# An encoder trunk in split float32: where the rounded high part of each weight comes from for the second sequence

## The chip, the cores and the metric

The kernel runs on one core of a Trainium2 chip. The metric is the device time of one execution in microseconds (us); a result is the median of several runs. The engines are TensorE (PE, with PEld for its weight loads), VectorE (DVE), ScalarE (ACT), GpSimd (POOL) and SyncE (SP). SP computes nothing here: its queue issues nearly all DMA transfers, in order, and waits before each until what the transfer needs is there.

## The reference

A trunk of two layers is applied to two requests of 512 tokens and 1024 channels, with one set of weights. Cut to what matters:

```python
def encoder_trunk(x, p):
    for l in range(DEPTH):                                   # 2
        h = rms_norm(x, p['ln1_g'][l])
        z = h @ p['w_in'][l]                                 # 1024 x 2816
        z_s5, z_hy, z_rw, z_na = jnp.split(z, IN_SPLITS, axis=-1)
        ...                                                  # four mixers, 256 channels each
        groups = [rms_norm(y, p['grp_g'][l, i]) for i, y in enumerate((y_s5, y_hy, y_rw, y_na))]
        x = x + jnp.concatenate(groups, axis=-1) @ p['w_out'][l]         # 1024 x 1024
        h = rms_norm(x, p['ln2_g'][l])
        x = x + jnp.square(jax.nn.relu(h @ p['w_mlp1'][l])) @ p['w_mlp2'][l]   # 1024 x 4096 x 1024
    return x

def reference(x_prompt, x_sample, ...):
    return (encoder_trunk(x_prompt, p), encoder_trunk(x_sample, p))
```

The mixers are a diagonal state-space scan (S5), a long convolution (Hyena), a linear-attention recurrence in two directions (RWKV-7) and 2-D neighbourhood attention.

## The kernel before

**Dense layers.** All tensors lie with channels on the 128 partitions and the 512 tokens of one sequence along the free dimension. To multiply with float32 accuracy, every operand is split: the high part is the value rounded to the matmul type float32r, the low part is what the rounding left. `mm3` (lines 1432 to 1434) makes three matmuls of 128x128 by 128x512 for each block: high weight by high activation, high weight by low activation, low weight by high activation. `dense` sums eight such blocks in one PSUM bank, `w_out` and `second` in `mlp` four or eight.

**Weights.** `load_w` brings four blocks, 128 x 512 float32 or 256 KB, so that one weight load serves 12 matmuls. A layer has 44 loads for `w_in`, 16 for `w_out`, and 128 for the two matrices of the MLP: 188, and 376 in the two layers. The first sequence meets each weight first, and the second meets it again later.

- First time (lines 1418 to 1422): SP loads the raw weights into a slot for low parts, ACT casts them into a slot for high parts (`split`, line 297), POOL, or VectorE for every fourth load, subtracts (line 298) and leaves the low part where the raw weights were, and SP writes the low part to DRAM (`lo`).
- Again (lines 1414 to 1416): SP loads the raw weights and the saved low part into two slots, and ACT casts the raw weights in place (line 1416).

There are seven slots of 256 KB. In the first case, three hold high parts and four hold low parts, in turn. In the second case, the loads take pairs of slots round the ring of seven. A slot is free when the matmuls that read it have ended, and a DMA that reads it too.

**Order.** Three streams of generators are interleaved: the dense layers of both sequences, the RWKV and S5 work with the other mixers, and the mixers of the very first sequence. A scheduler then orders the instructions of each engine, from a simulated time line and from priorities. The dense stream runs: `w_in` of layer 0 for sequence 0 (first time), for sequence 1 (again); `w_out`, MLP of layer 0 and `w_in` of layer 1 for sequence 0 (first time), the same for sequence 1 (again); `w_out` and MLP of layer 1 for sequence 0 (first time), and for sequence 1 (again). The last of these has no mixers beside it.

The profile's names: `m` is any SBUF buffer of the kernel's own allocator, weights among them; `pd` is the PSUM of the dense layers, `ra`, `ma` and `nm` that of the mixers and norms; `in_w_in`, `in_w_out` and `in_w_mlp` are the raw weights in DRAM, `lo` the saved low parts.

Of the kernel before, what the change touches and what calls it, by code (L numbers as in the profile page):

```python
# [5 lines left out]
F32 = mybir.dt.float32  # L6
F32R = mybir.dt.float32r
# [1392 lines left out]
def load_w(K, key):  # L1400


    nc = K.nc
    sh = [P, 4, P]
    src = K.A[key[0]][key[1:]]
    n = K.nw
    K.nw += 1
    again = key in K.lows
    i, j = (2 * n % NW, (2 * n + 1) % NW) if again else (n % NHI, NHI + n % (NW - NHI))
    hi, lo = (K.W.view(NMEM + 2 * o, sh, F32R) for o in (i, j))  # L1410
    raw = K.W.view(NMEM + 2 * (i if again else j), sh, F32)
    K.tc.cur_priority -= OFF_W
    if again:
        nc.sync.dma_start(out=raw, in_=src)
        nc.sync.dma_start(out=lo.bitcast(F32), in_=K.lows[key])
        nc.scalar.copy(out=hi, in_=raw)  # L1416
    else:
        nc.sync.dma_start(out=raw, in_=src)
        K.split(hi, lo, raw, nc.vector if K.nw % LO_V == 0 else nc.gpsimd)
        K.n += 1  # L1420
        d = K.lows[key] = K.d(sh, f"lo_{K.n}")
        nc.sync.dma_start(out=d, in_=lo.bitcast(F32))
    K.tc.cur_priority += OFF_W
    return hi, lo

# [12 lines left out]
def dense(K, key, h, tag="pd"):  # L1438

    w = [load_w(K, key + (kh,)) for kh in range(2)]  # L1440
    ps = K.p([P, S], tag)
    mm3(K, ps, [(w[k // 4][0][:, k % 4], w[k // 4][1][:, k % 4], h[k][0], h[k][1]) for k in range(8)])
    return ps
# [99 lines left out]
def w_out(K, l, khs, ys, xsrc, xp, done, M):  # L1543


    nc = K.nc
    load = not xp
    for m in range(8):
        if load and m % 2 == 0:
            xp.append(M([P, 2, S]))  # L1550
        x = xp[m // 2][:, m % 2]
        if load:
            nc.sync.dma_start(out=x, in_=xsrc[m * P:m * P + P])
        w = [load_w(K, ('w_out', l, m, kh)) for kh in khs]
        ps = K.p([P, S], "pd")
        mm3(K, ps, [(w[i][0][:, j], w[i][1][:, j]) + tuple(ys[HALVES[kh][j // 2]][:, part, j % 2] for part in range(2))
                    for i, kh in enumerate(khs) for j in range(4)])
        nc.vector.tensor_tensor(out=x, in0=ps, in1=x, op=ADD)
        if done:
            done(m, x, xp[m // 2])  # L1560
        yield
    M.free(*(ys.pop(g) for kh in khs for g in HALVES[kh]))


def mlp(K, l, h, R, x, done, M):
# [14 lines left out]
    def second(e):  # L1580
        for m in range(8):
            wh, wl = load_w(K, ('w_mlp2', l, m, e))
            ps = K.p([P, S], "pd")
            mm3(K, ps, [(wh[:, j], wl[:, j], hid[4 * e + j][:, 0], hid[4 * e + j][:, 1]) for j in range(4)])
            nc.vector.tensor_tensor(out=x[m], in0=ps, in1=x[m], op=ADD)  # L1585
            if e == 7:
                done(m, x[m])
            yield
        for j in range(4):
            M.free(hid.pop(4 * e + j))  # L1590
# [47 lines left out]
def trunk(tc, A, O):  # L1638
    nc = tc.nc
    base = place(nc)  # L1640
    with tc.tile_pool(name="sb", bufs=1) as sb, \
            tc.tile_pool(name="ps", bufs=1, space=bass.MemoryType.PSUM) as ps, \
            tc.tile_pool(name="dr", bufs=1, space=bass.MemoryType.DRAM) as dr:
        K = Ctx(tc, base, sb, ps, dr, A)
        K.s5w, K.hys, K.lows, K.nw, K.nz = {}, {}, {}, 0, 0
        K.W = K.mem()

        DM, MX = K.mem((0, DHI)), K.mem((DHI, NMEM))
# [170 lines left out]
NMEM, DHI, DLO, DS5 = 164, 84, 41, 144  # L1819

NW, NHI = 7, 3
# [49 lines left out]
```

## Time and profile before

| | |
|---|---|
| median of 3 runs | 3195.2 us (3182.29 to 3195.77) |
| the profiled execution | 3179.4 us, its span 3177.6 us |
| PE busy | 2951.0 us, 93% of the span |
| DVE, ACT, POOL busy | 1973.0, 1051.9, 828.9 us |
| casts of weights for the second sequence (line 1416) | 376, 232.8 us of ACT |
| DMA moved | 571.92 MB, a mean of 180 GB/s; 155.83 MB of it written to HBM |
| granted TensorE clock, mean | 0.95 |

Busy times overlap, so they don't add up to the span. Matmuls are pipelined, and one can be counted busy while the one before it still runs. What a stage is bound by is read from the stage: its PE idle time, its granted clock (1.00 is 2.4 GHz), its share of DMA time, and the waits that ended last.

### The profile page before, as it was taken

The page shows a single profiled execution, that of the slowest core. Times are in us where ns is not written, and L with a number is a line of the kernel's source. Part 1 is how long each engine was busy: PE and PEld are TensorE (multiplying, and loading weights), DVE is VectorE, ACT ScalarE, POOL GpSimd, SP SyncE. Part 2 cuts the span into 40 slices and gives each one's busy share as a digit, 9 for nine tenths or more (in the row PEclk, how much of TensorE's full clock was granted, in tenths as well). Part 3 has the DMA queues.
Part 4 walks back from the last instruction along what each step waited for, and adds up shares of the span by engine and source line. Part 5 has one row for each costly group of instructions (what it writes and reads, how often), then busy time and mean ns, then how long its engine had stood idle before and what let it go on. Part 6 is the DMA issues. An engine that isn't in the chain of part 4 may idle for free.

```text
span 3177.6 us, 48702 instructions
## 1 busy us (share of the span) xinstructions
PE 2951.0 (93%) x17328; PEld 2308.4 (73%) x17328; DVE 1973.0 (62%) x3755; ACT 1051.9 (33%) x1922; POOL 828.9 (26%) x693
## 2 busy tenths in 40 slices
PE   7987998798899998899899999998998999999999
PEld 5666776676677877767676778776776777778887
DVE  8888775785854768757627436765647457733332
ACT  5333233332322333333323223433322323332222
POOL 5642201432332336432001001312333223300000
PEclk9898999898999999999999999999999999999999
DMA  7577574365554546766655545577556445556565
GB/s 221 164 232 201 189 210 131 117 169 165 151 163 145 173 161 207 227 191 201 186 151 157 173 150 182 196 211 221 181 170 181 152 162 181 178 178 194 192 193 195
DMA packets 482840, 571.92 MB, mean 180 GB/s; under 512 B 187910, under 2 KB 238726, under 8 KB 481576
## 3 DMA queue, kind: packets, MB, share of 16 engines
q1 hardware_dynamic: 482600, 568.81, 58.4%
q8 instruction: 139, 2.28, 0.3%
q14 instruction: 101, 0.83, 0.1%
HBM read 409.95 MB, written 155.83 MB: 178 GB/s over the span
## 4 chain that ended last, share of the span: by engine, by line
PE 64%; DVE 16%; DMA 9%; issue 4%; SPq 3%; ACT 2%; POOL 1%; DVEq 0%; ACTq 0%; POOLq 0%
PE pd L1432 16%; PE pd L1434 16%; PE pd L1433 15%; DVE m L1195 2%; PE ra L677 2%; PE ra L675 2%; DMA m<-in_w_mlp 2%; PE ra L467 1%; DMA m<-in_w_in 1%; DVE m L864 1%; DVE m L530 1%; DVE m L298 1%; DMA m<-lo 1%; PE ra L1226 1%; PE ra L660 1%
## 5 line engine op out<-in xcount | busy, mean ns | idle before, releaser
L1432 PE MATMUL pd<-m,m 128*128 128x512 f32 x2984 | 1225.9, 412 | 91.7 <-ACT m L297 32.7
L1434 PE MATMUL pd<-m,m 128*128 128x512 f32 x2984 | 1210.2, 406 | 34.7 <-DMA m<-lo 23.6
L1433 PE MATMUL pd<-m,m 128*128 128x512 f32 x2984 | 1206.0, 404 | 2.3 <-DVE m L298 2.3
L1432 PEld LDWEIGHTS pd<-m,m 128*128 128x128 f32 x2984 | 580.4, 195 | 242.0 <-issue 46.0
L1434 PEld LDWEIGHTS pd<-m,m 128*128 128x128 f32 x2984 | 578.8, 194 | 176.0 <-DMA m<-lo 27.4
L1433 PEld LDWEIGHTS pd<-m,m 128*128 128x128 f32 x2984 | 580.6, 195 | 130.0 <-issue 8.0
L298 POOL TENSOR_TENSOR m<-m,m 128x512 fp32r<-128x512 f32 x282 | 395.7, 1405 | 736.5 <-ACT m L297 676.4
L1416 ACT CAST m<-m 128x512 fp32r<-128x512 f32 x376 | 232.8, 620 | 712.3 <-DMA m<-in_w_mlp 434.2
L297 ACT CAST m<-m 128x512 fp32r<-128x512 f32 (+1 forms) x400 | 256.9, 645 | 624.7 <-PE pd L1433 232.9
L1585 DVE TENSOR_TENSOR m<-pd,m 128x512 f32<-128x512 f32 x256 | 175.2, 686 | 262.6 <-PE pd L1434 262.2
L1575 DVE SCALAR_TENSOR_TENSOR do<-pd,R 128x512 f32<-128x512 f32 x128 | 87.7, 688 | 198.9 <-PE pd L1434 188.7
L1195 DVE TENSOR_TENSOR m<-m,m 128x512 f32<-128x512 f32 (+1 forms) x224 | 142.0, 677 | 4.5 <-POOL m L1195 3.6
L298 DVE TENSOR_TENSOR m<-m,m 128x512 fp32r<-128x512 f32 (+1 forms) x118 | 104.9, 889 | 62.9 <-ACT m L297 59.6
L298 DVE TENSOR_TENSOR m<-do,m 128x512 fp32r<-128x512 f32 x128 | 100.4, 786 | 62.1 <-ACT m L297 61.5
L297 ACT CAST m<-do 128x512 fp32r<-128x512 f32 x128 | 79.2, 620 | 137.0 <-DVE do L1576 136.8
L1576 DVE TENSOR_TENSOR do<-do 128x512 f32<-128x512 f32 x128 | 112.5, 880 | 3.0
L1456 POOL TENSOR_TENSOR m<-m 128x512 f32<-128x512 f32 x40 | 58.6, 1466 | 128.1 <-ACT m L1455 126.1
L1463 DVE SCALAR_TENSOR_TENSOR m<-m,par,m 128x512 fp32r<-128x512 f32 x64 | 65.1, 1026 | 34.2 <-ACT m L1462 34.1
L677 PE MATMUL ra<-m,m 128*64 128x64 f32 x512 | 77.8, 246 | 0.0
L1195 POOL TENSOR_TENSOR m<-m,m 128x512 f32<-128x512 f32 x32 | 49.2, 1540 | 98.1 <-DVE m L1195 54.9
L467 PEld LDWEIGHTS ra<-m,m 64*128 64x128 f32 x512 | 50.8, 201 | 32.5 <-issue 24.3
L675 PE MATMUL ra<-m,rw_st 64*64 64x64 f32 x448 | 73.8, 246 | 0.0
(359 smaller groups left out, 3489.9 us busy)
## 6 DMA issues: line engine op xcount, KB each, us to landing
m<-in_w_mlp SPq DMA_DIRECT2D x512, 256.0 KB, 2.9
lo<-m SPq DMA_DIRECT2D x376, 256.0 KB, 2.3
m<-lo SPq DMA_DIRECT2D x376, 256.0 KB, 2.7
m<-in_w_in SPq DMA_DIRECT2D x176, 256.0 KB, 3.5
m<-zr SPq DMA_DIRECT2D x36, 512.0 KB, 4.7
m<-in_w_out SPq DMA_DIRECT2D x64, 256.0 KB, 3.0
m<-in_xT SPq DMA_DIRECT2D x32, 256.0 KB, 4.5
zr<-do SPq DMA_DIRECT2D x32, 256.0 KB, 2.2
```

The costliest lines, as they stand in the source:

```text
L297: self.nc.scalar.copy(out=hi, in_=x)
L298: eng.tensor_tensor(out=lo, in0=x, in1=hi.bitcast(F32), op=SUB)
L675: nc.tensor.matmul(out=py[b0:b0 + 64, d, c], lhsT=st[b0:b0 + 64, d, c], rhs=ar[c][b0:b0 + 64, ch, 1], start=True, stop=False)
L677: nc.tensor.matmul(out=py[b0:b0 + 64, d, c], lhsT=uv[:, ch, c, q], rhs=sr[:, ch, 2 * c + q], start=st is None, stop=True)
L1195: eng.tensor_tensor(out=o, in0=a, in1=b, op=op)
L1416: nc.scalar.copy(out=hi, in_=raw)
L1432: K.nc.tensor.matmul(out=ps, lhsT=wh, rhs=hh, start=(i == 0), stop=False)
L1433: K.nc.tensor.matmul(out=ps, lhsT=wh, rhs=hl, start=False, stop=False)
L1434: K.nc.tensor.matmul(out=ps, lhsT=wl, rhs=hh, start=False, stop=(i == n - 1))
L1575: nc.vector.scalar_tensor_tensor(out=r, in0=ps, scalar=0.0, in1=R, op0=MAX, op1=MUL)
L1576: nc.vector.tensor_tensor(out=r, in0=r, in1=r, op=MUL)
L1585: nc.vector.tensor_tensor(out=x[m], in0=ps, in1=x[m], op=ADD)
```

## The change

The first sequence now writes both parts to DRAM, the high part (`hi`) as well as the low one, one store each on SP. The second sequence loads both parts from there and casts nothing. The raw weights are read once, by the first sequence. The slots and their order stay as they were: three and four in turn at the first time, pairs round the ring of seven again. The split of the first time is the same.

```diff
-    src = K.A[key[0]][key[1:]]
...
-    again = key in K.lows
-    i, j = (2 * n % NW, (2 * n + 1) % NW) if again else (n % NHI, NHI + n % (NW - NHI))
-    hi, lo = (K.W.view(NMEM + 2 * o, sh, F32R) for o in (i, j))
-    raw = K.W.view(NMEM + 2 * (i if again else j), sh, F32)
...
-    if again:
-        nc.sync.dma_start(out=raw, in_=src)
-        nc.sync.dma_start(out=lo.bitcast(F32), in_=K.lows[key])
-        nc.scalar.copy(out=hi, in_=raw)
+    if key in K.parts:
+        hi, lo = (K.W.view(NMEM + 2 * ((2 * n + i) % NW), sh, F32R) for i in range(2))
+        for t, d in zip((hi, lo), K.parts[key]):
+            nc.sync.dma_start(out=t.bitcast(F32), in_=d)
     else:
-        nc.sync.dma_start(out=raw, in_=src)
+        hi = K.W.view(NMEM + 2 * (n % NHI), sh, F32R)
+        o = NMEM + 2 * (NHI + n % (NW - NHI))
+        raw, lo = K.W.view(o, sh, F32), K.W.view(o, sh, F32R)
+        nc.sync.dma_start(out=raw, in_=K.A[key[0]][key[1:]])
         K.split(hi, lo, raw, nc.vector if K.nw % LO_V == 0 else nc.gpsimd)
         K.n += 1
-        d = K.lows[key] = K.d(sh, f"lo_{K.n}")
-        nc.sync.dma_start(out=d, in_=lo.bitcast(F32))
+        K.parts[key] = [K.d(sh, f"{p}_{K.n}") for p in ("hi", "lo")]
+        for t, d in zip((hi, lo), K.parts[key]):
+            nc.sync.dma_start(out=d, in_=t.bitcast(F32))
```

In the changed file the loads of the second sequence are line 1411, the raw load of the first is line 1416, both stores are line 1421, and the matmuls lines 1431 to 1433. SP's queue in the MLP of layer 1 for the first sequence, before (a name's last number only tells buffers apart):

```order
L1422 DMA lo_2191_23157<-m_23152 128x512
L1418 DMA m_23231<-in_w_mlp 128x512
L1422 DMA lo_2199_23202<-m_23197 128x512
L1418 DMA m_23239<-in_w_mlp 128x512
L1422 DMA lo_2203_23235<-m_23230 128x512
L1418 DMA m_23289<-in_w_mlp 128x512
```

And the changed kernel's, in the same stage:

```order
L1421 DMA hi_2519_23403<-m_23397 128x512
L1421 DMA lo_2520_23404<-m_23399 128x512
L1416 DMA m_23460<-in_w_mlp 128x512
L1421 DMA hi_2522_23413<-m_23407 128x512
L1421 DMA lo_2523_23414<-m_23409 128x512
L1416 DMA m_23470<-in_w_mlp 128x512
```

Load and store alternated; now a load is followed by the high and then the low part's store of the weight before it. In both, a raw load stands behind the low part's store of the weight two loads earlier.

ACT's queue near the end of the program, the MLP of layer 1 for the second sequence, before (line 1416 casts weights, line 297 the activations):

```order
L1416 CAST m_27787<-m_27789 128x512
L1416 CAST m_27793<-m_27795 128x512
L1416 CAST m_27830<-m_27832 128x512
L297 CAST m_27781<-do_27782 128x512
L1416 CAST m_27836<-m_27838 128x512
L1416 CAST m_27873<-m_27875 128x512
L297 CAST m_27824<-do_27825 128x512
```

And the changed kernel's, in that stage:

```order
L297 CAST m_27350<-do_27351 128x512
L297 CAST m_27533<-do_27534 128x512
L297 CAST m_27572<-do_27573 128x512
L297 CAST m_27611<-do_27612 128x512
L297 CAST m_27650<-do_27651 128x512
```

The casts of weights are gone from there, and the casts of activations follow each other.

## Rows read from the trace of the kernel before

**Rows 1.** The page, busy time, share of the span and instructions of PE.

```profile
PE 2951.0 (93%) x17328; PEld 2308.4 (73%) x17328; DVE 1973.0 (62%) x3755; ACT 1051.9 (33%) x1922; POOL 828.9 (26%) x693
```

**Rows 2.** Busy time by stretch, from : to and length in us; columns as headed.

```profile
core 0: us, PE busy (x) PEld busy (x) DVE busy (x) ACT busy (x) POOL busy (x), PEclk, DMA share, GB/s
0.00:221.00 221.00, 186.72 (x848) 135.84 (x849) 187.28 (x363) 87.58 (x144) 126.80 (x110) 0.94 0.67 202
221.00:475.00 254.00, 228.01 (x1659) 179.88 (x1657) 195.35 (x481) 87.55 (x173) 54.57 (x60) 0.91 0.70 204
475.00:1196.00 721.00, 655.06 (x4338) 508.41 (x4339) 474.65 (x870) 235.12 (x457) 229.28 (x177) 0.93 0.50 153
1196.00:1380.00 184.00, 160.69 (x833) 126.95 (x831) 143.14 (x253) 67.34 (x107) 94.58 (x84) 0.92 0.68 216
1380.00:2002.00 622.00, 593.40 (x3589) 456.72 (x3588) 346.09 (x690) 202.60 (x378) 80.37 (x75) 0.96 0.57 174
2002.00:2168.00 166.00, 154.10 (x792) 123.68 (x791) 112.06 (x221) 65.59 (x115) 31.94 (x27) 0.96 0.67 202
2168.00:2765.00 597.00, 570.96 (x3516) 445.58 (x3515) 380.93 (x676) 185.71 (x353) 204.86 (x157) 0.97 0.57 176
2765.00:3177.60 412.60, 402.02 (x1766) 331.35 (x1764) 133.49 (x204) 120.36 (x195) 6.47 (x5) 0.99 0.59 191
```

**Rows 3.** The page's costliest groups: busy us, mean ns | idle before, releaser.

```profile
L1432 PE MATMUL pd<-m,m 128*128 128x512 f32 x2984 | 1225.9, 412 | 91.7 <-ACT m L297 32.7
L1434 PE MATMUL pd<-m,m 128*128 128x512 f32 x2984 | 1210.2, 406 | 34.7 <-DMA m<-lo 23.6
...
L298 POOL TENSOR_TENSOR m<-m,m 128x512 fp32r<-128x512 f32 x282 | 395.7, 1405 | 736.5 <-ACT m L297 676.4
```

**Rows 4.** Line 1416: its casts (ns min/median/max), and who waited for them (us, times).

```profile
L1416 ACT CAST m<-m x376: 602/621/645, 225.5 to 3168.1; 128x512 fp32r<-128x512 f32 x188
...
  PE pd L1432: 9.9, 3
```

**Rows 5.** Line 1414, the raw loads again: who waited for them (us, times).

```profile
  ACT m L1416: 637.7, 298
```

**Rows 6.** Waits of PE, 221 to 475 us: total us, times, longest us.

```profile
PE pd L1434 <- DMA m<-lo: 10.3, 1, 10.3
...
PE ra L621 <- ACT m L610: 4.1, 1, 4.1
```

**Rows 7.** DMA queue, 2765 to 3177.6 us: packets, MB, share of 16 engines.

```profile
q1 hardware_dynamic: 43157, 78.57, 59.1%
```

**Rows 8.** DMA issues, 475 to 1196 us: count, KB, median us to landing.

```profile
m<-in_w_mlp SPq DMA_DIRECT2D x128, 256.0 KB, 2.8
```

**Rows 9.** DMA issues, 1196 to 1380 us.

```profile
m<-in_w_in SPq DMA_DIRECT2D x44, 256.0 KB, 3.5
lo<-m SPq DMA_DIRECT2D x44, 256.0 KB, 2.5
```

**Rows 10.** Waits of PE, 0 to 221 us.

```profile
PE pd L1432 <- ACT m L297: 17.0, 2, 13.1
PE pd L1434 <- POOL m L298: 3.2, 3, 2.2
...
PE ra L1434 <- POOL m L298: 2.0, 2, 1.7
```

**Rows 11.** Waits of PE, 1196 to 1380 us.

```profile
PE pd L1432 <- ACT m L297: 7.1, 3, 3.4
PE pd L1434 <- POOL m L298: 5.8, 3, 3.9
```

**Rows 12.** Waits of PE, 2168 to 2765 us.

```profile
PE pd L1432 <- ACT m L297: 8.3, 1, 8.3
```

**Rows 13.** Time line of SP, 2690 to 2695 us: start us, us, instruction.

```profile
2690.98 0.32 SPq L1422 DMA_DIRECT2D lo<-m  x1
```

**Rows 14.** Waits of SP's queue, whole span: total us, times, longest us.

```profile
SPq L1418 <- PE pd L1434: 333.4, 198, 12.7
SPq L1422 <- POOL m L298: 319.6, 207, 7.2
```

More of the change, by code (lines that the diff above doesn't have):

```diff
@@ L1644, in trunk @@
         K = Ctx(tc, base, sb, ps, dr, A)
-        K.s5w, K.hys, K.lows, K.nw, K.nz = {}, {}, {}, 0, 0
+        K.s5w, K.hys, K.parts, K.nw, K.nz = {}, {}, {}, 0, 0
         K.W = K.mem()
```

## Prediction

> **What bounds the kernel now.** I read the busy table first [rows 1]: TensorE (PE) is busy 2951.0 of 3177.6 us, so all its idle time is 226.6 us, and nothing that the change removes from another engine can return much more. Then the table by stretches [rows 2], cut at the first and last weight load of each stage. Stretches one, three, four and seven load weights for the first time (44, 144, 44 and 144 of them); two, five, six and eight load them again. The reader is to see three columns: PE idle (length less busy), the granted clock, and the DMA share. The last stretch, dense work alone, keeps PE busy 402.0 of 412.6 us at a clock of 0.99; there is little to win. The first-time stretches lose more: 23 us of 184 in the fourth.
>
> Third, who makes PE wait at the dense lines [rows 3]. Of the 91.7 + 34.7 us of idle time ahead of lines 1432 and 1434, casts of line 297 (the first sequence's, with those of the activations) end 32.7 us and the arrival of a saved low part 23.6 us. The second sequence's casts end only 9.9 us, in 3 waits out of 376 casts [rows 4]. In the last stretch 402.0 us for 1766 matmuls are 0.228 us each [rows 2], 2.73 us for the 12 matmuls of one weight load; that is the pace to which loads, casts and stores have to keep.
>
> **The change part by part.**
>
> *The casts go.* 376 casts of 0.62 us are 232.8 us of ScalarE (ACT), but 9.9 us of PE time [rows 4]. The high part now comes by the transfer that brought the raw weights: same size, same place on SP's queue, same slot. I take -10. The bounds are 0 and -34: the 23.6 us of waits for low parts would have to vanish as well. I leave them in, because the low-part load keeps its slot and its place behind the other load, and waits as before for the matmuls that release it.
>
> *ACT's queue is freed.* In front of those casts ACT sat 637.7 us waiting for raw weights [rows 5], and what stood behind them on ACT waited too. How much of that was ready to run, no row tells. The nearest row from below is one PE wait of 4.1 us for another ACT instruction in the second stretch [rows 6]. From above: PE's idle time in the four repeat stretches is 26.0 + 28.6 + 11.9 + 10.6 = 77.1 us [rows 2], and some of it lies on VectorE and DMA, so half of it, 38 us. I take -4, near the row that names ACT; bounds 0 and -38.
>
> *376 stores of 256 KB more, all in first-time stretches.* Their price on the DMA engines comes from the last stretch, where nearly all traffic is of this form: 59.1% of 412.6 us for 78.57 MB [rows 7] is 0.81 us of all 16 engines for 262,144 bytes. 44 stores are 36 us, 144 are 117 us. The DMA share then goes from 0.67 to 0.83 (first stretch), 0.50 to 0.66 (third), 0.68 to 0.87 (fourth) and 0.57 to 0.77 (seventh). At a share of 0.50 a raw weight lands in a median of 2.8 us, at 0.68 in 3.5 [rows 8, 9]. PE's waits for casts and subtractions are 7.1 + 5.8 = 12.9 us in the fourth stretch, and in the first 17.0 + 3.2 + 2.0 less one wait of 13.1 that I take for the start, 9.1 us [rows 10, 11]. Both stretches are near full afterwards, so I double these: +22. In the third and seventh, there is one such wait of note, 8.3 us in the seventh [rows 12]; the new ones are bounded below by no change, and above by the price of the fuller stretches, 22.0 / 88 = 0.25 us per load, on 288 loads: 72 us. I take +10, near the lower end. In the fourth stretch GpSimd (POOL), which makes three of four low parts, is busy 94.6 of 184 us with other work between; in the third and seventh it is busy a third of the time [rows 2], so weights stay further ahead. Together +32, bounds 0 and +94.
>
> By "HBM Reference" of the Trainium skill, section Specifications (TRN2), a core that streams alone reaches about 425 GB/s. This trace disagrees with such room: 216 GB/s already make 68% of the engines' time in the fourth stretch [rows 2], or 318 GB/s at full use. By the page, an estimate, the changed fourth stretch needs 216 GB/s and 11.53 MB in 184 us more, 279 GB/s, two thirds of that, no weight would come later than now, and the sum would be -14 in place of +18.
>
> *SP and the slots.* 376 more issues of 0.32 us [rows 13] are 120 us of SP's queue. The high part's store stands ahead of the low part's. SP already waits 319.6 us for POOL's subtractions before the low-part stores [rows 14], and the high part is ready one subtraction (1.4 us) sooner [rows 3]; so I price the issue at nothing. If that cover were gone, each raw load behind it would go out 0.32 us later. The store must land before the third cast after it reuses the slot: 2.5 us after issue in the fourth stretch [rows 9] against three weights of 2.73 us. Nothing either.
>
> The sum: -10 - 4 + 32 = +18 us. The profiled execution took 3179.4 us, so this one would take 3197.4. It lies 15.8 us under the median of the runs shown, 3195.2, and my number is for a median: **3213 us**.
>
> **The rivals.** *ACT was the hidden brake (faster).* If mixers' work was queued behind the waiting casts, half of the repeat stretches' idle time goes, 38 us with the casts' 10 in it, and the stores cost only 10: -28, 3167 us. For it: 637.7 us of blocked queue. Against it: ACT ends few of PE's waits [rows 3, 4]. It decides if ready ACT work stood behind a cast for over about a tenth of those 637.7 us and PE wanted its result.
>
> *The DMA engines have room (no change).* The stores land between other traffic and only -14 remains: 3181 us. For it: the second stretch runs at a share of 0.70, and low parts made PE wait there for 10.3 us in all, a single wait [rows 2, 6]. The rule of the Trainium skill named above describes this case.
>
> *The load loop closes (much slower).* A raw load goes out on SP only after the low-part store of the weight two before. So two weights take a landing (2.8), a cast (0.62), a subtraction (1.4) and two issues (0.64): 5.5 us, or 2.73 each [rows 3, 8, 13], just what 12 matmuls take. With landings of 3.5 us or more and a third issue it is 6.5 us, 3.3 each, 0.5 us over; other matmuls fill about half of that. Then the whole upper bound of +94 is paid: +80 net, 3275 us. Against it: SP waits 333.4 us for PE to free a slot before raw loads [rows 14], so loads are often early.
>
> *It doesn't do what it says.* If a cast of weights stayed in the second sequence, ACT's line would show it, and little would move: 3195 us.
>
> **How the numbers follow.** My forecast 0.40, ACT 0.22, DMA room 0.23, the loop 0.13, no effect 0.02. Three runs spread over 0.4%, so 0.5%, 16 us, is about what can be told from no change. +18 lies just beyond it, so 0.12 of the forecast falls inside; so does most of DMA room (-14), with 0.02 beyond. Faster 0.24, same 0.35, slower 0.41. The range reaches from -30 (the ACT case) to +80 (the loop): 3165 to 3275. Stalls also cost clock: the stretches with the largest share of idle time, one to four, were granted 0.91 to 0.94, a mean over the levels of 2.4 and 1.2 GHz, and the last 0.99 [rows 2]; that is why the range is longer upwards. The scheduler's order shifts a little everywhere; I price that at nothing.
>
> **What would show it.** No weight casts on ACT in the repeat stretches, and PE's 9.9 us gone. Written bytes up by 98.6 MB. DMA shares near 0.83, 0.66, 0.87 and 0.77 in the first-time stretches, raw loads landing in 3.5 to 4 us in the first and fourth, and PE's waits for line 297 and the subtractions up by some 30 us. I am wrong if these landings stay where they are, if the repeat stretches shrink by over 20 us, or if the third and seventh grow by more than the first and fourth.

## The result, and the profile after

The changed kernel takes 3218.3 us, the median of five runs (3212.1 to 3219.9), beside 3195.2 for the kernel before (five runs, 3182.3 to 3197.0). The ratio is 1.0075, with a 95% interval of 1.0050 to 1.0099: 23 us slower. The prediction said 3213, +18.

The profiled execution took 3217.5 us. First the page's busy time, the queue that carries the loads and stores, and the bytes.

```profile
span 3215.8 us, 48528 instructions
...
PE 2979.9 (93%) x17328; PEld 2324.8 (72%) x17328; DVE 1973.2 (61%) x3755; ACT 826.1 (26%) x1546; POOL 831.9 (26%) x693
...
q1 hardware_dynamic: 536744, 667.40, 66.6%
...
HBM read 409.95 MB, written 254.39 MB: 207 GB/s over the span
```

ACT runs 376 instructions less, 1546 instead of 1922, and is busy 225.8 us less. Written bytes rose by 254.39 - 155.83 = 98.56 MB, which is 376 stores of 262,144 bytes. So the change does what it says. PE runs the same 17328 instructions as in [rows 1], yet it is busy 28.9 us longer, and idle 3215.8 - 2979.9 = 235.9 us instead of 226.6. Of the 38.2 us by which this span exceeds the earlier one, three quarters are the same matmuls taking longer. Such a difference of two profiles is rough: two profiles of the kernel before (the second stands below) differ by 18.3 us of span and 11.1 us of PE time.

The table by stretch, cut as in [rows 2], shows with what they go together.

```profile
core 0: us, PE busy (x) PEld busy (x) DVE busy (x) ACT busy (x) POOL busy (x), PEclk, DMA share, GB/s
0.00:233.00 233.00, 194.11 (x868) 141.44 (x869) 196.08 (x369) 89.12 (x147) 124.41 (x111) 0.92 0.77 244
233.00:478.00 245.00, 222.15 (x1634) 174.17 (x1633) 195.14 (x481) 61.15 (x127) 57.63 (x58) 0.92 0.72 208
478.00:1241.00 763.00, 687.91 (x4397) 531.00 (x4396) 485.15 (x888) 236.67 (x462) 235.65 (x179) 0.90 0.62 195
1241.00:1433.00 192.00, 158.07 (x778) 120.23 (x777) 134.50 (x239) 67.10 (x106) 99.95 (x89) 0.89 0.82 264
1433.00:2033.00 600.00, 585.02 (x3623) 452.41 (x3623) 349.41 (x700) 118.37 (x243) 73.09 (x69) 0.98 0.59 180
2033.00:2197.00 164.00, 154.50 (x760) 124.42 (x759) 107.04 (x204) 37.53 (x61) 31.25 (x27) 0.95 0.70 208
2197.00:2803.00 606.00, 574.33 (x3507) 448.76 (x3507) 370.75 (x671) 183.00 (x352) 203.50 (x157) 0.95 0.74 233
2803.00:3215.80 412.80, 403.80 (x1773) 332.39 (x1772) 135.13 (x206) 33.19 (x52) 6.46 (x5) 0.99 0.60 194
```

In all four first-time stretches (one, three, four, seven) the DMA share is up by 0.10 to 0.17 and the granted clock, a mean over the levels of 2.4 and 1.2 GHz, is down by 0.02 or 0.03. The fifth, a repeat, has a higher clock than before, 0.98 for 0.96. The lengths themselves mislead: the third is 42 us longer, but its PE count went from 4338 to 4397 and the fourth's from 833 to 778. The scheduler moved work between them. The last four experiments below hold the order for that reason.

What PE waits for at line 1431 and 1433 (1432 and 1434 before), by the page's groups:

```profile
L1431 PE MATMUL pd<-m,m 128*128 128x512 f32 x2984 | 1226.5, 412 | 95.5 <-ACT m L297 54.8
L1433 PE MATMUL pd<-m,m 128*128 128x512 f32 x2984 | 1208.3, 406 | 23.6 <-POOL m L298 13.3
```

Casts of line 297 now end 54.8 us of idle time ahead of the high part's matmul instead of 32.7 [rows 3]; ahead of the low part's, it is no longer the saved low part that ends most, but POOL's subtraction. By stretch, PE's waits for the first sequence's casts and subtractions, first 0 to 233 us (total us, times, longest us):

```profile
PE pd L1431 <- ACT m L297: 20.2, 4, 12.6
...
PE pd L1433 <- POOL m L298: 3.0, 6, 0.8
...
PE ra L1431 <- ACT m L297: 0.6, 1, 0.6
```

478 to 1241 us:

```profile
PE pd L1431 <- ACT m L297: 8.4, 4, 4.9
```

1241 to 1433 us:

```profile
PE pd L1431 <- ACT m L297: 10.8, 2, 7.3
...
PE pd L1433 <- POOL m L298: 7.1, 5, 4.5
```

2197 to 2803 us:

```profile
PE pd L1431 <- ACT m L297: 12.6, 3, 9.6
...
PE pd L1433 <- POOL m L298: 1.5, 1, 1.5
```

They answer to [rows 10 to 12]. The first stretch hardly moved (23.8 us, 22.2 before), the fourth went from 12.9 to 17.9, the seventh from 8.5 (with a wait of 0.2 for a subtraction) to 14.1; in the third, the waits for casts went from 0.4 to 8.4. Part of this is the new order, as the experiments show.

Raw loads land later. DMA issues of the first and of the fourth stretch (count, KB each, median us to landing):

```profile
m<-in_w_in SPq DMA_DIRECT2D x44, 256.0 KB, 4.3
```

```profile
m<-in_w_in SPq DMA_DIRECT2D x44, 256.0 KB, 4.1
```

In the fourth it was 3.5 before [rows 9], in the first 3.3. And SP's queue over the whole span, which now waits before a store in two ways:

```profile
SPq L1416 <- PE pd L1433: 270.5, 162, 11.3
SPq L1421 <- ACT m L297: 200.6, 165, 4.3
SPq L1421 <- POOL m L298: 176.9, 181, 4.6
```

The 319.6 us that SP waited for POOL [rows 14] are now split between the cast (before the high part's store) and the subtraction (before the low part's), and together they are longer: 377.5.

### The profile page after: what moved, and what is told of

It reads as the page before. It is cut to its first block, busy times and chain, and to the rows that moved or that the text cites. A ratio compares the mean times of both kernels' runs of the same rounds, so it can differ in the third digit from the quotient of the medians.

```text
span 3215.8 us, 48528 instructions
## 1 busy us (share of the span) xinstructions
PE 2979.9 (93%) x17328; PEld 2324.8 (72%) x17328; DVE 1973.2 (61%) x3755; ACT 826.1 (26%) x1546; POOL 831.9 (26%) x693
## 3 DMA queue, kind: packets, MB, share of 16 engines
HBM read 409.95 MB, written 254.39 MB: 207 GB/s over the span
## 4 chain that ended last, share of the span: by engine, by line
PE 40%; DVE 6%; DMA 3%; issue 1%; ACT 1%; SPq 1%; POOL 0%; ACTq 0%; DVEq 0%; POOLq 0%
PE pd L1431 11%; PE pd L1433 11%; PE pd L1432 10%; DVE m L1195 1%; PE ra L677 1%; PE ra L675 1%; DMA m<-in_w_mlp 1%; PE ra L467 1%; DVE m L530 1%; PE ma L1344 0%; PE ra L1226 0%; DVE m L1584 0%; PE ra L1276 0%; DVE m L512 0%; DVE m L437 0%
## 5 line engine op out<-in xcount | busy, mean ns | idle before, releaser
L1431 PE MATMUL pd<-m,m 128*128 128x512 f32 x2984 | 1226.5, 412 | 95.5 <-ACT m L297 54.8
L1433 PE MATMUL pd<-m,m 128*128 128x512 f32 x2984 | 1208.3, 406 | 23.6 <-POOL m L298 13.3
L1455 POOL TENSOR_TENSOR m<-m 128x512 f32<-128x512 f32 x40 | 57.3, 1432 | 104.4 <-ACT m L1454 104.4
L467 PE MATMUL ra<-m,m 64*128 64x128 f32 x512 | 59.4, 304 | 19.4 <-DVE m L451 7.0
L862 POOL TENSOR_TENSOR m<-m,s5p_i 128x256 f32<-128x256 f32 x64 | 54.5, 851 | 69.1 <-DVE m L864 38.2
## 6 DMA issues: line engine op xcount, KB each, us to landing
hi<-m SPq DMA_DIRECT2D x376, 256.0 KB, 3.1
lo<-m SPq DMA_DIRECT2D x376, 256.0 KB, 2.9
m<-hi SPq DMA_DIRECT2D x376, 256.0 KB, 3.1
m<-lo SPq DMA_DIRECT2D x376, 256.0 KB, 2.7
m<-in_w_mlp SPq DMA_DIRECT2D x256, 256.0 KB, 3.1
m<-in_w_in SPq DMA_DIRECT2D x88, 256.0 KB, 4.2
m<-in_xT SPq DMA_DIRECT2D x32, 256.0 KB, 4.8
```

The lines of the kernel that those rows point to most:

```text
L467: nc.tensor.matmul(out=pm[q][:, ch - c2, c], lhsT=bk[c][h, ch].rearrange("p a b -> p (a b)"), rhs=ar[c][h, ch].rearrange("p a b -> p (a b) ...
L1431: K.nc.tensor.matmul(out=ps, lhsT=wh, rhs=hh, start=(i == 0), stop=False)
L1433: K.nc.tensor.matmul(out=ps, lhsT=wl, rhs=hh, start=False, stop=(i == n - 1))
```

## The experiments

Times are medians in us; a ratio is to the kernel before on the same chip and stands with its 95% interval. The kernel before took 3196.6 beside the first four experiments, 3198.6 beside the next three, and 3198.7 or 3198.8 beside the last four. In the first seven the scheduler was free to order each version anew.

### Each half alone

**Stores only.** The kernel before, with the high part written to DRAM too and read by nobody.

```diff
         d = K.lows[key] = K.d(sh, f"lo_{K.n}")
+        nc.sync.dma_start(out=K.d(sh, f"hi_{K.n}"), in_=hi.bitcast(F32))
         nc.sync.dma_start(out=d, in_=lo.bitcast(F32))
```

> The kernel before, with the high part's store added in the first sequence and read by nobody; the second sequence casts as before. Theory (the stores' DMA time delays the raw loads and drops the clock in the first-time stretches, and is worth more than the 23 us of the whole change, because the repeat stretches gained some 33 us): 45 to 70 us over before, 3240 to 3265 us, with first-time stretches as long as the changed kernel's. Rival (the order that the scheduler writes, not the stores, made the third stretch 42 us longer): within 15 us of before, 3180 to 3210 us. Prediction as written (+32): 3227 us.

Measured: 3221.5, ratio 1.0065 [1.0039, 1.0091], +25. That lies under the theory and above the rival, nearest to the prediction's +32.

**No cast, no stores.** The second sequence loads two parts and casts nothing.

```diff
     if again:
-        nc.sync.dma_start(out=raw, in_=src)
+        nc.sync.dma_start(out=hi.bitcast(F32), in_=K.lows[key])
         nc.sync.dma_start(out=lo.bitcast(F32), in_=K.lows[key])
-        nc.scalar.copy(out=hi, in_=raw)
```

> The kernel before, whose second sequence loads two parts and casts nothing, while the first sequence stores only the low part; what is loaded in the high part's place is a second copy of the low part, so the second sequence is computed without the high part of its weights. It shows what the casts cost alone, with no store added. Theory (ACT's queue was worth more than the 14 us that I took): 25 to 40 us under before, 3155 to 3170 us. Prediction as written: 3181 us. Rival (the repeat stretches got shorter only because mixer work had moved into the third stretch): within 8 us of before.

Measured: 3180.3, ratio 0.9948 [0.9925, 0.9970], -16. This is the only kernel of the study that is faster than the one before, and it leaves out the high part of the second sequence's weights. So the casts were worth 16 us, near the prediction's 14 and under the theory's 25, and the stores cost more than that. Its order was the scheduler's own too; a pair with the order held, below, gives the same.

### Which part of a store costs

**The high part's store on ACT's queue.** The changed kernel; SP issues only the low part's store.

```diff
-        for t, d in zip((hi, lo), K.parts[key]):
-            nc.sync.dma_start(out=d, in_=t.bitcast(F32))
+        for t, d, q in zip((hi, lo), K.parts[key], (nc.scalar, nc.sync)):
+            q.dma_start(out=d, in_=t.bitcast(F32))
```

> The changed kernel, with the high part's store issued from ACT's queue right behind its cast, and not from SP's. Same bytes, same slots; SP no longer waits for a cast and issues 376 transfers fewer. Theory (DMA time): 3210 to 3225 us, as the change. Rival (SP's order: the raw loads stand behind the high part's store on SP): the cost of the stores is gone, 3165 to 3185 us.

Measured: 3218.6, ratio 1.0070 [1.0049, 1.0090], the same as the change. SP's extra issues, and its waits for casts, are not what makes the change slow; or ACT pays as much for them.

**Small stores.** The first experiment, with 4 KB stored in place of 256 KB.

```diff
+        nc.sync.dma_start(out=K.d(sh, f"hi_{K.n}")[:, :1, :8], in_=hi[:, :1, :8].bitcast(F32))
```

> The run with stores only, but each store writes 32 bytes per partition, 4 KB in place of 256 KB. Issues, waits and order on SP stay, the bytes go. Theory (DMA time): within 10 us of before, 3185 to 3205 us. Rival (SP's order, or the slot that waits for its store): as the run with full stores, 3240 us or more.

Measured: 3230.5, ratio 1.0103 [1.0079, 1.0128], +34. A sixty-fourth of the bytes cost no less than all of them. The theory missed. Taken alone, this says that bytes are free and the issue or its wait is dear.

**A store that waits for nothing.** The same 4 KB out of a tile that is set once, so that nothing is waited for and no slot is held.

```diff
+        nc.sync.dma_start(out=K.d(sh, f"hi_{K.n}")[:, :1, :8], in_=K.cst)
...
+        K.cst = K.t([P, 1, 8], "cst")
+        nc.gpsimd.memset(K.cst, 0.0)
```

> The run with small stores, but what is stored is a constant tile of 4 KB: 376 more issues on SP, which wait for no cast and hold no slot of the high parts. Theory (the store's wait for the cast on SP, or the slot that is held until it lands, is the cost): within 8 us of before, 3185 to 3205 us. Rival (376 more issues on SP, wherever they wait, are the cost): as with small stores, 3222 to 3240 us.

Measured: 3220.2, ratio 1.0075 [1.0053, 1.0097], +22. The theory missed again. Even 376 issues that wait for nothing and hold nothing seem to cost as much as the change. What these kernels have in common is that the scheduler, given a longer program, writes another order.

**Another order without added work.** The kernel before, with VectorE's turn (each fourth subtraction) two loads later.

```diff
-        K.split(hi, lo, raw, nc.vector if K.nw % LO_V == 0 else nc.gpsimd)
+        K.split(hi, lo, raw, nc.vector if K.nw % LO_V == 2 else nc.gpsimd)
```

> The kernel before with another one of every four subtractions on VectorE (load 3 of 4 and not 4 of 4): the same work, another order from the scheduler. Theory (order alone is worth little): within 8 us of before. Rival (the order before is a lucky one, and any other costs as much as the stores do): 3215 to 3235 us.

Measured: 3222.3, ratio 1.0083 [1.0059, 1.0108], +24, as much as the whole change, and as the rival said. The edit also changes which subtractions VectorE makes; this run doesn't part that from the order. So the three results above don't price a store. An edit that lets the scheduler choose again can be off by its own size.

**Eight slots.** The changed kernel with a fourth slot for high parts (the pairs of the repeat loads stay on a ring of seven).

```diff
-        hi, lo = (K.W.view(NMEM + 2 * ((2 * n + i) % NW), sh, F32R) for i in range(2))
+        hi, lo = (K.W.view(NMEM + 2 * ((2 * n + i) % NA), sh, F32R) for i in range(2))
...
-NW, NHI = 7, 3
+NW, NHI, NA = 8, 4, 7
```

> The changed kernel with eight weight slots, four of them for high parts in the first sequence (three before); the second sequence goes round seven as it did. Theory that the high part's slot, held until its store has landed, holds back the casts: 3185 to 3200 us, most of the cost of the stores gone. Rival (the slot is not it; SP's waits or the order are): 3210 to 3225 us, as the change.

Measured: 3227.8, ratio 1.0099 [1.0077, 1.0121], +29. The trace shows that ACT's casts waited for stores, and that the wait is gone. Line 1421's waiters (both stores), in the change and with eight slots (us, times):

```profile
  ACT m L297: 46.3, 16
```

```profile
  ACT m L297: 2.7, 2
```

Of the 46.3 us, the trace names a high part's store in 5 waits (15.6 us) and a low part's in 11 (30.7 us). The kernel did not get faster, so the theory missed: ACT's wait for a held slot is off the path, or the new order took back what it gave.

**The kernel before, once more.** A second profile of the same kernel, since the first profile lay 16 us under the median of its runs.

> The kernel before once more, for a second profile of it: the first profiled execution, 3179.4 us, lies some 17 us under the median of the runs since. Theory (the first profile caught a lucky third stretch): 3190 to 3200 us, with the third stretch (w_out and MLP of layer 0, first sequence) 10 to 20 us longer than in the first profile and more of it at the low clock. Rival (the third stretch is as short in every run): within 5 us of the first profile there.

Measured: 3197.7, beside its median of 3198.6, inside the theory's range. Cut at nearly the same matmuls, the first profile's third stretch is 720.7 us and this one's 727.4, its fifth 620.2 and this one's 627.5: the difference is spread, and the third stretch's part is under the theory's 10 us. What goes with the time from run to run is the granted clock: the 66 runs of the kernel before beside these experiments reach from 3173.2 us at a mean clock of 0.955 to 3216.5 at 0.941. The second profile serves below as the one to compare with. Its eight stretches, with cuts some microseconds away from those of [rows 2], at matmuls that the kernels of the next part share:

```profile
0.00:231.00 231.00, 197.98 (x925) 143.28 (x926) 194.82 (x378) 91.13 (x150) 128.62 (x113) 0.93 0.67 205
231.00:489.50 258.50, 227.90 (x1692) 177.67 (x1692) 193.02 (x473) 85.15 (x170) 55.22 (x58) 0.92 0.70 201
489.50:1216.90 727.40, 659.48 (x4270) 510.38 (x4271) 483.38 (x877) 238.38 (x462) 235.46 (x179) 0.93 0.49 150
1216.90:1399.00 182.10, 159.36 (x817) 124.37 (x815) 135.68 (x245) 66.33 (x105) 90.23 (x83) 0.92 0.70 224
1399.00:2026.50 627.50, 597.29 (x3594) 461.54 (x3594) 349.85 (x698) 203.39 (x382) 79.75 (x75) 0.95 0.56 170
2026.50:2193.30 166.80, 155.35 (x794) 124.14 (x794) 111.68 (x212) 63.84 (x111) 32.38 (x27) 0.96 0.68 203
2193.30:2786.60 593.30, 565.73 (x3503) 440.81 (x3503) 378.22 (x682) 184.39 (x352) 205.09 (x156) 0.97 0.56 175
2786.60:3195.90 409.30, 399.02 (x1744) 328.81 (x1742) 131.13 (x193) 119.11 (x193) 6.45 (x5) 0.99 0.59 190
```

### The same with the order held

At the end of the program, each engine's instructions are tied in a given order, by edges that only the scheduler sees and that put no wait into the program. `_ORDER` holds, for each engine, the order of the kernel before (or, in the second experiment here, of the stores-only kernel). The added stores are left out of it in the first and third.

```diff
+        pin(K)
...
+def pin(K):
+    ins = {}
+    for i in K.nc.cur_bb.bb.instructions:
...
+            ins.setdefault(str(i.engine).split(".")[-1], []).append(i)
+    for e, packed in _ORDER.items():
...
+        for a, b in zip(order, order[1:]):
+            K.tc.add_manual_dep(ins[e][b], ins[e][a].name,
+                                mybir.DependencyInfo(mybir.DependencyClass.NoSync, mybir.DependencyReason.DATA),
+                                reason="order")
```

**Stores in the old order.** The stores-only edit, all else in the order of the kernel before.

> The kernel before with the high parts' stores, read by nobody, and with every other instruction held in the order of the kernel before on each engine (ordering edges without semaphores, from a table); the scheduler places the stores alone. Theory now (the order that the scheduler writes costs the time, the stores' bytes, issues and slots next to nothing): 3195 to 3208 us, of which the first stretch some 8 us longer from the DMA traffic. Rival (the stores themselves cost it): 3215 to 3230 us, as with stores in an order of their own.

Measured: 3235.1, ratio 1.0120 [1.0095, 1.0144], +36, above theory and rival both.

**No stores in the new order.** The kernel before, its work in the order that the scheduler chose for the stores-only kernel.

> The work of the kernel before, no store added, held on each engine in the order that the scheduler wrote for the run with stores only. Theory (order): 3212 to 3226 us, with a third stretch of 755 to 770 us. Rival (the stores): within 8 us of before, 3189 to 3205 us, third stretch 720 to 730 us.

Measured: 3196.1, ratio 1.0000 [0.9979, 1.0020]. That order costs nothing by itself, to within 0.2%. Between it and the stores-only kernel only the stores differ, and those are 25 us there. The idea that the order alone makes the change slow has fallen; what the order does is move the price of the stores, between 25 and 36 us in these two.

**The whole change in the old order.** The casts out, the stores in, all that remains as it stood.

> The whole change, held on each engine in the order of the kernel before (the casts of line 1416 left out of it, the high parts' stores placed by the scheduler). Theory (order): the gain of the run without casts and stores, -16, and a few us for the stores: 3178 to 3192 us, faster than both kernels. Rival (the stores): 3205 to 3220 us.

Measured: 3219.2, ratio 1.0067 [1.0044, 1.0091], +20. That is 15.9 us below stores alone in the same order; the casts, taken out without any stores, gave 16.3. The two halves add up. In orders of their own they don't: +25 and -16 make +9, and the change took +23.

**Small stores in the old order.** As the first of these four, with every store at the same place in SP's queue, but 4 KB each.

> The run with stores in the old order, every instruction on every engine in the same place, SP's stores of high parts too; each of these 376 stores writes 4 KB in place of 256 KB. Theory (DMA time, as predicted): the 36 us of the full stores nearly gone, 3195 to 3208 us. Rival (the issues, SP's waits for a cast in front of raw loads, and the held slot, whatever the bytes): 3222 to 3240 us.

Measured: 3210.0 (12 runs, 3191.5 to 3234.4), ratio 1.0038 [1.0014, 1.0062], +11. Its interval stands clear of the full stores' 1.0095 to 1.0144. It missed the theory by 2 us and the rival by 12. In the traces, VectorE, ScalarE, GpSimd, SP and the matmuls of both kernels follow the same sequence. So bytes make 3235.1 - 3210.0 = 25 us of the 36, and 376 issues with their packets, waits and held slots the other 11. The queue that carries them, full and small stores (packets, MB, share of 16 engines):

```profile
q1 hardware_dynamic: 536744, 667.40, 66.0%
```

```profile
q1 hardware_dynamic: 536744, 570.38, 58.3%
```

The packets are as many; the bytes raise the share from 58.3% to 66.0%. ACT's casts waited for high parts' stores in both, full and small (us, times):

```profile
  ACT m L297: 28.3, 10
```

```profile
  ACT m L297: 25.9, 11
```

So the 25 us are not in that wait. Which of issue, packets, wait and slot makes the 11 stays open. The profiled execution of the small stores was their longest, at a clock of 0.936, so its stretches aren't read.

The bytes show in how long a store takes. Medians from issue to landing of full stores in the old order, and of the low parts beside small ones:

```profile
hi<-m SPq DMA_DIRECT2D x376, 256.0 KB, 3.1
lo<-m SPq DMA_DIRECT2D x376, 256.0 KB, 3.0
```

```profile
lo<-m SPq DMA_DIRECT2D x376, 256.0 KB, 2.3
```

And by stretch, lengths in us, where the PE counts of all three agree to within one (a single profile of each):

| stretch | before, second profile | stores, old order | change, old order |
|---|---|---|---|
| 1, first time | 231.0 | 238.3 (+7.3) | 236.5 (+5.5) |
| 2, again | 258.5 | 256.0 (-2.5) | 250.2 (-8.3) |
| 3, first time | 727.4 | 746.0 (+18.6) | 745.1 (+17.7) |
| 4, first time | 182.1 | 189.0 (+6.9) | 191.0 (+8.9) |
| 5, again | 627.5 | 621.5 (-6.0) | 610.5 (-17.0) |
| 6, again | 166.8 | 168.5 (+1.7) | 164.4 (-2.4) |
| 7, first time | 593.3 | 612.1 (+18.8) | 607.7 (+14.4) |
| 8, again | 409.3 | 407.7 (-1.6) | 406.3 (-3.0) |

The first-time rows of the stores in the old order:

```profile
0.00:238.30 238.30, 202.92 (x925) 145.24 (x926) 192.78 (x378) 91.50 (x153) 126.90 (x113) 0.91 0.79 246
...
494.30:1240.30 746.00, 670.94 (x4270) 517.00 (x4271) 481.75 (x878) 238.26 (x462) 236.37 (x179) 0.91 0.63 198
1240.30:1429.30 189.00, 161.92 (x818) 123.97 (x816) 134.65 (x245) 64.78 (x103) 89.90 (x83) 0.91 0.83 270
...
2219.30:2831.40 612.10, 572.33 (x3503) 445.46 (x3503) 375.15 (x682) 183.97 (x352) 202.47 (x156) 0.96 0.73 231
```

Length less busy gives PE idle of 35.4, 75.1, 27.1 and 39.8 us, against 33.0, 67.9, 22.7 and 27.6 in the second profile. So of the 51.6 us that these stretches grew, idle time is 26.0 and longer busy time of the same matmuls 25.6, at a clock that is lower by 0.01 or 0.02 in each. In the change in the old order it is 16.0 of 46.5.

How much of the price is clock, these profiles don't settle: the execution with stores had a mean clock of 0.939, that of the kernel before 0.949. Runs that were granted the same, 0.943 to 0.946, took 3195 to 3208 us in the kernel before (13 runs beside the last four experiments), 3200 to 3210 with small stores (7) and 3233 to 3236 with full ones (3). At the same mean clock, then, the full stores still cost 34 us by medians, and 28 of these are bytes.

Nor is the growth mostly in the waits that I had named. PE's waits for casts and subtractions in the four first-time stretches are 50.6 us in the second profile and 57.8 with stores in the old order. The casts' part in the third and in the seventh stretch, before:

```profile
PE pd L1432 <- ACT m L297: 0.4, 1, 0.4
```

```profile
PE pd L1432 <- ACT m L297: 11.3, 3, 8.5
```

With the stores in the old order:

```profile
PE pd L1433 <- ACT m L297: 3.3, 5, 1.1
```

```profile
PE pd L1433 <- ACT m L297: 11.2, 3, 8.3
```

The dense matmuls' waits for VectorE's other results grew more, from 36.4 to 48.3 us, and the rest is spread over the mixers. The loads do come later: the raw weights of the MLP landed in a median of 3.2 us in the third stretch and 3.4 in the seventh, in both 2.8 before.

The fifth stretch, a repeat, with the casts and without (stores in the old order, then the change in the old order):

```profile
1429.30:2050.80 621.50, 593.17 (x3593) 458.24 (x3594) 349.08 (x698) 203.89 (x384) 78.66 (x75) 0.96 0.57 173
```

```profile
1422.80:2033.30 610.50, 587.34 (x3594) 454.31 (x3594) 350.17 (x698) 119.89 (x243) 80.97 (x75) 0.97 0.58 176
```

Without casts it has 23.2 us of idle time instead of 28.3, and its matmuls are busy 5.8 us less at a clock of 0.97 instead of 0.96. Here less waiting and a higher clock go together.

## Why the prediction was right, and where it was not

The sum stands. +18 was forecast and +23 measured, +20 in the held order; the stores were put at +32 and cost 36, the casts with ACT's queue at -14 and gave 16. The steps inside it stand less well, and that the stores came so near is in part luck: one term of theirs was too high, one too low, and SP with the slots was put at nothing.

- **The casts go: -10, and ACT's queue: -4.** Measured together: -16, by two pairs of kernels, one of them with the order held. The waits that the casts ended were 9.9 us [rows 4]; where the rest came from isn't shown. I had left in the waits for saved low parts, 23.6 us [rows 3]. In the changed kernel they are shorter. Who waited for the loads of line 1411 (us, times; line 1433 reads the low part):

```profile
  PE pd L1433: 10.0, 3
```

  But that is the new order: with the order held they stayed. The loads of low parts in the second profile of the kernel before, and those of line 1411 in the change in the old order:

```profile
  PE pd L1434: 24.0, 7
```

```profile
  PE pd L1435: 22.2, 9
```

  So that step was right. In the two profiles with the order held, the repeat stretches shrank by 22 us between stores alone and the whole change (30.7 less 8.4). My mark of "over 20 us" was passed in single profiles, in the direction of the rival in which ACT is the hidden brake; the timed effect of 16 is under half of that rival's 38.
- **The stores: +22 in the first and fourth stretch, +10 in the third and seventh.** The size was right, the place and the path were not. In the held order the first and fourth grew by 14.2 us, the third and seventh by 37.4, which is what I had named as showing me wrong. Per load that is 14.2 / 88 = 0.16 us and 37.4 / 288 = 0.13 us: nearly the same price everywhere. I had taken the full stretches at 0.25 and the others at 0.035, on the argument that PE's waits for casts and subtractions mark where a later weight costs, and that the third and seventh had but one such wait. The step that failed is that argument: with the order held these waits grew by 7.2 us, while the stretches grew by 51.6. The rest is other waits, for VectorE's results above all, and the same matmuls busy for longer. By what way the bytes cause these is open.
- **The signs.** DMA shares of 0.83, 0.66, 0.87 and 0.77 were expected; they are 0.77, 0.62, 0.82 and 0.74, lower because the stretches became longer, and because a store took less: in the first stretch 0.77 of 233 us is 31 us more than 0.67 of 221, for 44 stores, 0.71 us each and not 0.81, which was the price of loads. Raw loads landed in 4.3 and 4.1 us, a little over the 3.5 to 4 expected. PE's waits for line 297 and the subtractions were to grow by some 30 us; in the four first-time stretches they went from about 48 us to 66, so by 18, of which the held order shows 7.
- **SP and the slots: nothing.** This failed. Issues, packets, waits and slots without the bytes cost 11 us (1.0038, with an interval that excludes 1). The cover that I named, a landing of 2.5 us against three weights, broke: in the old order ACT's casts waited 10 times for a high part's store, 28.3 us in all. Taking such waits away with an eighth slot, or the issue from SP, did not make the change faster, but both had orders of their own, so what exactly is paid there is open.
- **The order: nothing.** Right on balance, for this change (+20 in the old order, +23 in its own), but not a safe price: +24 for two loads' difference in whose turn a subtraction is, and +34 against +11 for small stores in their own and in the old order.

*The rivals.* That the DMA engines have room, falls: the bytes alone cost 25 us, at 246 to 270 GB/s in the first and fourth stretch. By "HBM Reference" of the Trainium skill, Specifications (TRN2), 425 GB/s are there for a core that streams alone; the runs disagree with what I had worked out from that, that no weight would come later (raw loads of the fourth stretch landed in 4.1 us, not 3.5): the measurement decides. That the load loop closes, falls too (its 6.5 us for two weights are 3.24 each, not 3.3): nothing near +80 was seen, and SP still waits 270.5 us for PE before raw loads, so loads are still often early. The ACT brake is real at less than half its size.

No version tried computes everything and beats the kernel before. The missing casts need the high parts in DRAM, and writing them costs 36 us in the held order where the casts left out save 16.

## What to carry to other kernels

A store that no one waits for still slows the loads beside it, and the whole program with them; price its bytes wherever the DMA engines are busy, also where the trace shows no waits for weights. Set against it not the saved engine's busy time, 232.8 us here, but what the program gained when the casts went alone, 16. Where a scheduler orders the instructions, an edit's time is the edit and a new order; hold the order before the edit is priced, above all when tens of microseconds in three thousand are at stake. One profile can lie half a per cent under the median of its kernel: take a second profile before stretches are subtracted, and compare the granted clocks of the two.

## What the runs showed that I had not expected

- Moving every fourth subtraction by two loads cost 24 us (1.0083), without an instruction more, as much as 98.6 MB of stores did.
- 4 KB stores cost more than 256 KB stores when the scheduler was free (+34 and +25), and a third of them when it was not (+11 and +36).
- By profiles with the order held, a 256 KB store cost 0.16 us per load in the two stretches whose DMA share had been 0.67 and 0.70, and still 0.13 in the two with 0.49 and 0.56.
- PE's instructions were the same in number, and yet three quarters of the span's growth between the two profiles shown was PE being busy for longer: 28.9 us, with the mean granted clock at 0.94 instead of 0.95. Runs of the kernel before differ by as much in clock.
